# Plain products for the first four column blocks, longer load runs and spread weight copies in a Strassen-like ReGLU MLP

## The chip, the cores and the metric

The kernel runs on one core of one Trainium2 chip (trn2). The metric is the device time of a run in microseconds (us), lower is better; runs of one kernel agree within about 1%. The profiled execution of a kernel is one of its runs; its span is about 1.8 us shorter than that run's time. PE is TensorE, DVE is VectorE, ACT is ScalarE, POOL is GpSimd and SP is SyncE; PEclk is the granted TensorE clock, 1.0 being full speed. The views print 1.00 until the first change of clock that a trace records, so at the very start the matmul times tell more than PEclk. A load "lands" when its transfer has finished.

## The reference, cut to what matters

```python
# x: (16, 256, 512), w1: (512, 4096), w2: (2048, 512), all float32
h = x @ w1
gate, value = np.split(h, 2, axis=-1)
h = np.maximum(gate, 0) * value
return (h @ w2).astype(np.float32)
```

## The kernel before

The 4096 tokens go in four sets of 1024. A set is cut into two token halves (512 each); the 512 input features are cut into two halves; and w1 into gate and value. So the first layer is a 2 x 2 by 2 x 2 block product, done per column block of 128 hidden columns with seven products (P1 to P7) instead of eight. One product is two matmuls of 128x128 by 128x512. Its operands are sums: S1 to S4 of blocks of x, T1 to T4 of blocks of w1. A set has 16 such column blocks, and then the second layer: 8 output tiles of 16 matmuls. The last four matmuls of a set's second layer are spread into the next set's first blocks.

While the second layer of a set runs, x of the next set is loaded, transposed by DVE in 32x32 squares, and summed by POOL. This is where the change and the argument touch:

```python
stage = ctx.enter_context(tc.tile_pool(name="stage", bufs=3))    # x half tiles and w1 tiles, 4 KB each
tmp = ctx.enter_context(tc.tile_pool(name="tmp", bufs=4))
psx = ctx.enter_context(tc.tile_pool(name="psx", bufs=3, space=bass.MemoryType.PSUM))   # X and O
...
def load_x(s, h, k):                    # half a token half: 512 KB in four transfers, runs of 256 B
    t = stage.tile([P, 16, 64], F32, name="xs", tag="stage")
    for q in range(4):
        nc.sync.dma_start(out=t[q * 32:(q + 1) * 32], in_=x_v[s, h, k, q])
    return t

def turn(t):                            # reads t with a step of 2 floats (8 bytes)
    a = tmp.tile([P, 2, TH], F32, name="xt", tag="tmp")
    nc.vector.transpose(a.rearrange("p b (tb r) -> p b tb r", r=32),
                        t.rearrange("p tb (c b) -> p b tb c", b=2))
    return a

def x_ops(s, eng):
    o = x_tiles()
    t11 = load_x(s, 0, 0)
    t21 = load_x(s, 1, 0)
    yield o                             # each yield: ten matmuls of the second layer are issued
    a11 = turn(t11)
    nc.scalar.copy(out=o["A11"], in_=a11)
    t22 = load_x(s, 1, 1)
    yield o
    a21 = turn(t21)
    eng.tensor_tensor(o["S3"], a11, a21, op=SUB)
    t12 = load_x(s, 0, 1)
    yield o
    a22 = turn(t22)
    eng.tensor_tensor(o["S1"], a21, a22, op=ADD)
    nc.scalar.copy(out=o["A22"], in_=a22)
    yield o
    ...                                 # A12, S2, S4
...
def mm2_stream(s, g):                   # second layer
    for b in range(NB):
        ps = psx.tile([P, DO], F32, name="O", tag="X")
        for hc in range(NJ):
            nc.tensor.matmul(ps, g[:, hc, b * P:(b + 1) * P], w2_sb[:, hc, :],
                             start=hc == 0, stop=hc == NJ - 1)
            if hc < NJ - 1:
                yield
        o = tmp.tile([P, DO], F32, name="o", tag="tmp")
        nc.scalar.copy(out=o, in_=ps)   # in order on ACT, between the copies of x_ops
        nc.sync.dma_start(out=out_v[s, b], in_=o)
        yield
...
# opening: all of x_ops(0, ...) on DVE, w1 block 0 and 1 prepared, only then the first set's products
gen = x_ops(0, nc.vector)
xo = next(gen)
ws = {0: load_w1(0)}
next(gen)
w1_ops(0, ws[0], nc.vector)
for _ in gen:
    pass
...
```

The second layer's output tiles take their PSUM buffers from a pool of three (`psx`). A tile can start only when ACT has copied the tile three places before it. So whatever stands ahead of such a copy in ACT's queue can stop PE.

## Time and profile before

| Before | us |
|---|---|
| time, median (range) of 4 runs | 351.01 (350.92 to 352.05) |
| span of the profiled execution | 351.2 |
| sum of PE work without any wait: 64 blocks x 3.21 + 512 matmuls x 0.216 | 316 |
| start: until 26.0 us only 16 matmuls are done | 22 lost |
| two stops in blocks 11 and 12, and half clock until block 13 (counted from 0) | 8.7 lost |
| end: last matmul to end of span | 3.6 |

These are lines of the page of the kernel before. The first three are the busy tenths of PE, its granted clock and the DMA engines in 40 equal slices of 8.8 us. Then come groups of instructions (engine, operation, count, busy time, mean ns of one, idle time before them) and DMA issues (KB of one, median us from issue to landing).

```profile
PE   3259996799999999999999999999999999999995
PEclk9559999789999999999999999999999999999999
DMA  9957689920821700000821700000721000000212
...
L81 DVE STREAM_TRANSPOSE xt<-xs 128x1024 f32<-128x1024 f32 x16 | 19.5, 1234 | 25.0 <-DMA xs<-in_x_dram 17.6
...
xs<-in_x_dram SPq DMA_DIRECT2D x64, 128.0 KB, 3.3
...
w_sb<-in_w_dram POOLq DMA_DIRECT2D x4, 512.0 KB, 13.1
```

PE is short of work in the first three slices, around the seventh and eighth, and in the last. The view of waits, restricted to PE, names what ended each stop (total us, times, longest):

```profile
PE X L144 <- ACT Y L151: 9.2, 3, 4.0
PE W L144 <- DVE x_S_110 L104: 6.1, 1, 6.1
PE X L144 <- ACT w_B_81 L125: 4.0, 1, 4.0
```

Of the first line, one stop of 4.0 us lies at the start and two (2.97 and 2.25 us) in blocks 11 and 12 (the three slow blocks are 11 to 13 counted from 0; the prediction below calls them 10 to 12). The timeline of PE shows the start: start time, duration, instruction, and in brackets the idle time before it.

```profile
9.18 1.22 PE L144 MATMUL X<-x_A_107,w_B_81 128*128 128x512 f32 x2 [4.00 <-ACT w_B_81 L125]
16.47 1.19 PE L144 MATMUL W<-x_S_110,w_T_84 128*128 128x512 f32 x2 [6.07 <-DVE x_S_110 L104]
21.62 1.01 PE L144 MATMUL X<-x_A_108,w_B_82 128*128 128x512 bf16 x2 [3.96 <-ACT Y L151]
```

The first product runs at 9.18 us, the second must wait for S1 (a sum that needs A21 and A22), and the third for ACT's copy of the first one's result, which ran only at 20.99 us, behind copies of x and w1 in ACT's queue. Now the boundary between the first two sets, in the timeline of DVE. The second layer of the first set starts at 81.57 us.

```profile
85.58 2.36 DVE L81 STREAM_TRANSPOSE xt<-xs 128x1024 f32<-128x1024 f32 x2
92.25 1.25 DVE L81 STREAM_TRANSPOSE xt<-xs 128x1024 f32<-128x1024 f32 x1 [4.32 <-DMA xs<-in_x_dram]
```

A11 and A21 are both transposed at once, because both halves had been loaded long before. Only the third and fourth loads are issued here (87.41 us), and the third lands at 92.25. The output copies on ACT wait little, and PE has no gap at any boundary.

### The profile page before, as it was taken

The numbers are of one execution on the slowest core, as the hardware profiler recorded it, in microseconds if no ns is written. First come the engines' busy times: TensorE is split into PE (matmuls) and PEld (weight loads), VectorE is DVE, ScalarE is ACT, GpSimd is POOL, SyncE is SP. The second block draws the span as 40 slices with busy tenths as digits, with TensorE's granted clock in tenths as the row PEclk, the third lists the DMA queues.
The fourth block names the chain that finished last, engine by engine and source line by source line (L and its number), as shares of the span: only waits on it lengthen the run. The fifth ranks groups of instructions, "written<-read, shape, count | busy, mean of one in ns | idle before, by whom it ended". The sixth has DMA issues, their size and how long they took to land.

```text
span 351.2 us, 4077 instructions
## 1 busy us (share of the span) xinstructions
PE 326.3 (93%) x1416; PEld 204.5 (58%) x1416; DVE 195.1 (56%) x285; ACT 153.9 (44%) x285; POOL 71.7 (20%) x76
## 2 busy tenths in 40 slices
PE   3259996799999999999999999999999999999995
PEld 1137774575445777775445777775445777775442
DVE  2877786368201778778201788778111788776000
ACT  2277775443234455543233455543233455552121
POOL 0068996520540000000540000000460000000000
PEclk9559999789999999999999999999999999999999
DMA  9957689920821700000821700000721000000212
GB/s 164 194 156 201 184 181 213 205 62 0 179 105 46 149 0 3 0 1 2 179 96 55 149 0 0 2 1 0 182 97 54 32 0 0 0 2 0 91 68 81
DMA packets 57940, 27.53 MB, mean 78 GB/s; under 512 B 35392, under 2 KB 53824, under 8 KB 57920
## 3 DMA queue, kind: packets, MB, share of 16 engines
q1 hardware_dynamic: 55808, 25.18, 28.1%
q0 software_dynamic: 2112, 2.10, 3.6%
q8 instruction: 11, 0.18, 0.2%
q14 instruction: 9, 0.07, 0.1%
HBM read 20.97 MB, written 8.39 MB: 84 GB/s over the span
## 4 chain that ended last, share of the span: by engine, by line
PE 79%; DMA 7%; POOL 6%; SPq 3%; issue 2%; DVE 1%; ACT 0%; POOLq 0%; DVEq 0%; ACTq 0%
PE O L188 32%; PE Y L144 21%; PE W L144 14%; PE X L144 13%; DMA ws<-in_w_dram 7%; SPq L118 2%; POOL w_T_87 L131 1%; POOL w_T_85 L128 1%; POOL w_T_86 L130 1%; SPq L76 1%; POOL w_T_84 L126 1%; POOL w_sb L240 1%; DVE xt L81 1%; DVE x_S_110 L104 0%; ACT Y L151 0%
## 5 line engine op out<-in xcount | busy, mean ns | idle before, releaser
L188 PE MATMUL O<-w_sb,g 128*128 128x512 bf16 x512 | 113.6, 379 | 0.0
L171 DVE TENSOR_TENSOR cc<-W,pu 128x512 f32<-128x512 f32 x64 | 44.3, 692 | 89.6 <-ACT pu L165 82.6
L188 PEld LDWEIGHTS <-g 128*128 128x128 bf16 x512 | 48.7, 98 | 61.1 <-issue 4.9
L165 ACT COPY pu<-Y 128x512 f32<-128x512 f32 x64 | 37.6, 587 | 46.6 <-PE Y L144 46.6
L151 ACT COPY Y<-X 128x512 f32<-128x512 f32 x64 | 36.7, 574 | 43.6 <-PE X L144 43.6
L193 ACT COPY o<-O 128x512 f32<-128x512 f32 x32 | 18.8, 586 | 70.4 <-PE O L188 65.9
L172 DVE SCALAR_TENSOR_TENSOR g<-X,cc 128x512 bf16<-128x512 f32 x64 | 44.2, 691 | 2.4
L181 DVE SCALAR_TENSOR_TENSOR g<-Y,cc 128x512 bf16<-128x512 f32 x64 | 43.5, 680 | 3.4 <-PE Y L144 3.4
L177 DVE TENSOR_TENSOR cc<-Y,pu 128x512 f32<-128x512 f32 x64 | 43.6, 681 | 3.1 <-PE Y L144 3.1
L158 ACT COPY pu<-W 128x512 f32<-128x512 f32 x64 | 37.5, 586 | 0.5 <-PE W L144 0.3
L81 DVE STREAM_TRANSPOSE xt<-xs 128x1024 f32<-128x1024 f32 x16 | 19.5, 1234 | 25.0 <-DMA xs<-in_x_dram 17.6
L144 PEld LDWEIGHTS <-w_B_82 128*128 128x128 bf16 x128 | 7.9, 98 | 26.6 <-issue 25.9
L144 PE MATMUL X<-x_A_108,w_B_82 128*128 128x512 bf16 x32 | 10.1, 398 | 9.2 <-ACT Y L151 9.2
L144 PE MATMUL W<-x_S_110,w_T_84 128*128 128x512 f32 x32 | 11.4, 443 | 6.1 <-DVE x_S_110 L104 6.1
L100 POOL TENSOR_TENSOR x_S_1397<-xt 128x1024 fp32r<-128x1024 f32 x1 | 2.3, 2342 | 66.5 <-DVE xt L81 66.5
L100 POOL TENSOR_TENSOR x_S_2016<-xt 128x1024 fp32r<-128x1024 f32 x1 | 2.4, 2351 | 66.3 <-DVE xt L81 66.3
L126 POOL TENSOR_TENSOR w_T_84<-ws 128x256 fp32r<-128x256 f32 x14 | 10.4, 746 | 26.2 <-DMA ws<-in_w_dram 26.2
L144 PE MATMUL X<-x_A_107,w_B_81 128*128 128x512 f32 x32 | 11.8, 456 | 4.0 <-ACT w_B_81 L125 4.0
L144 PE MATMUL Y<-x_S_111,w_T_85 128*128 128x512 f32 x32 | 13.6, 506 | 0.0
L144 PE MATMUL Y<-x_S_777,w_T_85 128*128 128x512 f32 x32 | 13.0, 487 | 0.0
L144 PE MATMUL Y<-x_S_2015,w_T_85 128*128 128x512 f32 x32 | 13.0, 487 | 0.0
L144 PE MATMUL Y<-x_S_1396,w_T_85 128*128 128x512 f32 x32 | 13.0, 487 | 0.0
(92 smaller groups left out, 466.6 us busy)
## 6 DMA issues: line engine op xcount, KB each, us to landing
xs<-in_x_dram SPq DMA_DIRECT2D x64, 128.0 KB, 3.3
ws<-in_w_dram SPq DMA_DIRECT2D x64, 128.0 KB, 2.7
out_dram<-o SPq DMA_DIRECT2D x32, 256.0 KB, 2.0
w_sb<-in_w_dram POOLq DMA_DIRECT2D x4, 512.0 KB, 13.1
```

The lines of the kernel that those rows point to most:

```text
L81: nc.vector.transpose(a.rearrange("p b (tb r) -> p b tb r", r=32), t.rearrange("p tb (c b) -> p b tb c", b=2))
L126: eng.tensor_tensor(op["T1"], b12, b11, op=SUB)
L144: nc.tensor.matmul(ps, wop[wn][:, b, self.jb * P:(self.jb + 1) * P], self.xo[xn][:, b, :], start=fresh and b == 0, stop=b == 1, skip_group ...
L151: nc.scalar.copy(out=self.Y, in_=self.X)
L158: nc.scalar.copy(out=self.p5, in_=self.W)
L165: nc.scalar.copy(out=self.u2, in_=self.Y)
L171: nc.vector.tensor_tensor(self.c12, self.W, self.u2, op=ADD)
L172: nc.vector.scalar_tensor_tensor(out=self.g[:, self.jb, :TH], in0=self.X, scalar=0.0, in1=self.c12, op0=MAX, op1=MULT)
L177: nc.vector.tensor_tensor(self.c22, self.Y, self.p5, op=ADD)
L181: nc.vector.scalar_tensor_tensor(out=self.g[:, self.jb, TH:], in0=self.Y, scalar=0.0, in1=self.c22, op0=MAX, op1=MULT)
L188: nc.tensor.matmul(ps, g[:, hc, b * P:(b + 1) * P], w2_sb[:, hc, :], start=hc == 0, stop=hc == NJ - 1)
L193: nc.scalar.copy(out=o, in_=ps)
```

## The change

The intent: shorten the start. Four column blocks of the first set use the eight plain products, which need only copies of x and w1, so that PE can start as soon as half of x is there and the sums are made meanwhile. x comes in 1 MB loads of 512-byte runs and w1 in pairs of blocks with 1 KB runs; the first set's second x load is staged in the idle space of g, and w1 in the idle space of w2, so w2 must load after all of w1. 38 warm-up matmuls hold the clock until x is there. The last output tile is split between ACT and DVE. To make this fit, x staging shrinks to one buffer of 8 KB (a whole token half), and `x_ops` is rewritten for it.

```diff
-    stage = ctx.enter_context(tc.tile_pool(name="stage", bufs=3))
-    tmp = ctx.enter_context(tc.tile_pool(name="tmp", bufs=4))
+    stage = ctx.enter_context(tc.tile_pool(name="stage", bufs=1))
+    tmp = ctx.enter_context(tc.tile_pool(name="tmp", bufs=5))
...
-    x_v = x2.rearrange("(s h tb r) (k q c) -> s h k q r tb c", h=2, tb=16, r=32, k=2, q=4)
+    x_v = x2.rearrange("(s h tb r) (q c) -> s h q r tb c", h=2, tb=16, r=32, q=4)
...
-    def turn(t):
-        a = tmp.tile([P, 2, TH], F32, name="xt", tag="tmp")
+    def turn(a, t, k):
         nc.vector.transpose(a.rearrange("p b (tb r) -> p b tb r", r=32),
-                            t.rearrange("p tb (c b) -> p b tb c", b=2))
+                            t.rearrange("p tb (c k b) -> p k b tb c", k=2, b=2)[:, k])
         return a
+
+    def x_tile():
+        return stage.tile([P, 16, P], F32, name="xs", tag="xs")
...
         o = x_tiles()
-        t11 = load_x(s, 0, 0)
-        t21 = load_x(s, 1, 0)
+        t1 = load_x(s, 0, x_tile())
         yield o
-        a11 = turn(t11)
+        a11 = turn(x_tmp(), t1, 0)
         nc.scalar.copy(out=o["A11"], in_=a11)
-        t22 = load_x(s, 1, 1)
+        a12 = turn(x_tmp(), t1, 1)
+        nc.scalar.copy(out=o["A12"], in_=a12)
+        t2 = load_x(s, 1, x_tile())
         yield o
-        a21 = turn(t21)
+        a21 = turn(x_tmp(), t2, 0)
+        a22 = turn(x_tmp(), t2, 1)
+        eng.tensor_tensor(o["S1"], a21, a22, op=ADD)
         eng.tensor_tensor(o["S3"], a11, a21, op=SUB)
-        t12 = load_x(s, 0, 1)
-        yield o
-        a22 = turn(t22)
-        eng.tensor_tensor(o["S1"], a21, a22, op=ADD)
         nc.scalar.copy(out=o["A22"], in_=a22)
         yield o
...
+    class Plain:
+        def products(self, h, a1, a2):
+            ...
+            for a, gate, value in ((a1, "B11", "T3"), (a2, "T4", "B22")):
+                for ps, wn in ((X, gate), (W, value)):
+                    for b in range(2):
+                        nc.tensor.matmul(ps, wop[wn][:, b, js], a[:, b, :], start=a is a1 and b == 0,
+                                         stop=a is a2 and b == 1)
...
+    fetch(0, nc.scalar)
+    t1 = load_x(0, 0, x_tile())
+    fetch(1, nc.sync)
+    fetch(2, nc.sync)
+    t2 = load_x(0, 1, late)             # late: the space of g's blocks 12 to 15
+    ...
+    plain[0].products(0, r11, r12)
+    ...                                 # plain blocks 0 to 3 for half 0, then for half 1,
+    plain[3].products(1, r21, r22)      # with S1 to S4 (DVE) and T1 to T4 (POOL) made between them
```

## The prediction

> **What bounds it now.** TensorE: in the windows view it is busy without a gap from 110 us on. One block (14 products) takes 3.21 us in the timeline, one second-layer matmul 0.216 us (114 in 24.6 us in the chain of waits), so 64 blocks and 512 matmuls need about 64 x 3.21 + 512 x 0.216 = 316 us. The other 35 us:
> - start: by 26.0 us only 16 matmuls (3.7 us) are done: 22 us lost. PE waits for four x loads, transposes and sums, and for w1, all behind SP's issues, partly at half clock;
> - blocks 10 to 12: two stops behind a w1 load that took 12 us beside the w2 load (usually 2.7), then half clock: 18.3 us for three blocks, 8.7 lost;
> - end: last matmul at 347.6, then copy, issue, landing: 3.6 us.
>
> **What the change does.**
> 1. Plain blocks need only A11/A12, then A21/A22, and w1 copies: no sums before the first product. Cost: 64 matmuls instead of 56, fp32r at 0.231: +2.0 us; ideal 318 us.
> 2. First w1 on ACT's queue, x in 1 MB loads of 512-byte runs, w1 in 1 MB pairs of 1 KB runs. The first two loads are 1.5 MB; estimated at 200 to 250 GB/s (before: 199 at 512-byte runs, DMA share 0.7), landed by 7.5 to 9 us. Transpose 1.24 + copy 1.04: first operand at 10 to 11.5. The Trainium skill ("DMA: Bandwidth & Descriptors", Specifications) puts line rate at 512 bytes and up; the 256-byte x loads here ran at 218 GB/s with DMA share over 1, which agrees.
> 3. 38 warm-up matmuls from 2.0 us: some 9 at 0.427, 29 at about 0.22: until 12.2 us. The skill ("TensorE: Matmul & The Clock Gate", Part 1) has about 3.4 us of activity before full clock; the trace agrees (restart 21.6, full at 25.0). Real work starts near 12.4 us, warm.
> 4. w1 is staged in w2's space, so w2 loads after all w1: the 8.7 us stop goes. POOL needs an estimated 1.3 us per 128x512 operation (0.745 for 256, 2.35 for 1024 columns), 5.3 a pair, under PE's 6.4. w2 is issued at 54 to 57 us and lands by 70, just as the second layer needs it.
> 5. Last output in halves: 0.2 to 0.5 us.
>
> **New waits.** (a) Half 1 of the plain blocks needs the second x load, 4 MB into the queue (17 to 20 us), then transposes and copies: 0 to 3 us. (b) Copies of w1 pairs stand in ACT's queue and wait for loads whose buffer was just freed: 1 to 2 us around blocks 4 to 6. (c) At each set boundary x staging has one buffer: the second load starts after the first is transposed, and the A22 copy precedes the second output copy on ACT. PE needs that PSUM buffer 15 us after the second layer starts, the copy comes at about 16: 1 us, three times.
>
> **Sum.** 12.4 + 318 + 3.2 (end) + 2.5 (a, b, w2) + 3 (c) = 339 us, 3.4% faster; range 335 to 344. Faster by over 2%: 0.90; within 2%: 0.09; slower: 0.01.
>
> **Right if** the first plain product starts at 11.5 to 14 us at granted clock 1.0; set 1 starts near 97 us, not 109; no w1 landing of 12 us; no PE gap between 50 and 65 us; POOL's sums at a boundary end 23 us after the second layer starts.
>
> **Wrong if** warm-up ends before x has landed and the clock falls again; the longer runs load no faster; w2 comes late (each us after 70 adds one); the boundary waits are 3 us, or none.

## The result, and the profile after

The changed kernel is correct and slower. Its median is 367.5 us (366.71 to 369.32, 4 runs) against 351.01 us of the kernel before (4 runs): ratio 1.047, 95% interval 1.0426 to 1.0514. A ratio here is the mean time of one kernel's runs over the mean of the other's runs of the same rounds, so it is not quite the ratio of the two medians. The predicted 339 us, with a range of 335 to 344, was wrong, and on the wrong side of 351.

Here are the lines of the page of the changed kernel that answer to those shown before. Line L218 is the second layer, and L87 is the transpose.

```profile
PE   7969999996799999999499999999589999999995
PEclk9999999999699999999899999999969999999998
DMA  9973687905225000006132400001422000000212
...
L218 PE MATMUL O<-w_sb,g 128*128 128x512 bf16 x500 | 120.5, 396 | 16.6 <-ACT o L230 16.0
...
L87 DVE STREAM_TRANSPOSE xt<-xs 128x1024 f32<-128x1024 f32 x14 | 27.5, 2000 | 28.5 <-DMA xs<-in_x_dram 28.5
...
L227 DVE COPY o<-O 128x256 f32<-128x256 f32 x1 | 0.4, 425 | 25.2 <-ACT o L225 25.2
...
xs<-in_x_dram SPq DMA_DIRECT2D x28, 256.0 KB, 4.9
...
w_sb<-in_w_dram POOLq DMA_DIRECT2D x4, 512.0 KB, 9.2
```

The start is full but for the third slice (7 9 6, the waits of the plain blocks below), and it is warm (at full clock): the timeline has the first product at 13.00 us, and from 15.91 us on each pair of matmuls follows the one before by 0.46 us. The stop in the seventh and eighth slices of before is gone. But three dips have come, at slices 10-11, 20 and 29-30. They are the set boundaries. The second layer's group now has 16.6 us of idle time, before it had 0.0. One transpose takes 2.0 us where it took 1.24. The view of waits puts all the waiting at the boundaries on one line (16.0 us in three stops); the next two are the largest waits of the first set's plain blocks:

```profile
PE O L218 <- ACT o L230: 16.0, 3, 5.4
...
PE X L206 <- ACT x_A_182 L302: 1.3, 1, 1.3
PE X L206 <- ACT x_S_185 L299: 1.1, 1, 1.1
```

"ACT o" is the copy of an output tile, but that copy takes only 0.58 us. What it stood behind is told by the chain of waits through the first boundary (start, duration, what), followed back from a second-layer matmul:

```profile
77.90 4.04 DVE xt L87 x2
...
81.96 0.31 SPq L83
...
83.37 5.22 DMA xs<-in_x_dram
...
88.67 3.86 DVE xt L87 x2
...
92.56 1.05 ACT x_A_707 L116
...
93.64 0.46 ACT o L230
...
94.14 4.00 PE O L218 x9
```

Read from the top: the first x half, long landed, is transposed twice. Only then is the single staging buffer free, so the second load is issued at 81.96 and lands at 88.67. Two more transposes follow, then the copy of A22 on ACT, and only behind it, in ACT's queue, the copy of output tile 1. PE needed the buffer of that tile for output tile 4 at 88.93 and got it at 94.14: a gap of 5.21 us, in the timeline of PE:

```profile
94.14 15.70 PE L218 MATMUL O<-w_sb,g 128*128 128x512 bf16 x59 [5.21 <-ACT o L230]
```

In the windows view (stretch, its length, then busy us and count of PE, PEld, DVE, ACT and POOL, then clock, DMA share and GB/s) the clock falls late in the gap and is still at half after it (by the trace's clock record from 92.58 to 99.41 us):

```profile
90.00:92.00 2.00, 0.00 (x0) 0.00 (x0) 2.00 (x2) 0.00 (x0) 0.00 (x0) 1.00 0.00 0
92.00:94.20 2.20, 0.06 (x1) 0.06 (x1) 0.52 (x1) 1.53 (x2) 1.53 (x1) 0.63 0.00 0
94.20:96.00 1.80, 1.80 (x5) 0.63 (x5) 0.00 (x0) 0.58 (x1) 1.80 (x2) 0.50 0.39 146
96.00:98.00 2.00, 2.00 (x7) 0.66 (x5) 0.00 (x0) 0.58 (x1) 2.00 (x2) 0.50 0.35 131
```

The 59 matmuls that follow take 15.70 us, where 59 x 0.216 is 12.7. The other two boundaries have gaps of 5.38 and 5.39 us, and 59 matmuls in 14.78 and 15.98 us.

The loss can be added up from the times at which sets start. The table compares the stretches with those of before:

| Stretch (us) | Before | After |
|---|---|---|
| first product | 9.18 | 13.00 |
| start of the first set's second layer | 81.57 | 73.95 |
| from there to the start of set 1 | 27.63 (to 109.20) | 35.53 (to 109.48) |
| set 1 to set 2 | 79.18 (to 188.38) | 86.28 (to 195.76) |
| set 2 to set 3 | 79.01 (to 267.39) | 87.51 (to 283.27) |
| set 3 to the end of the span | 83.8 | 84.2 |

The change gains 7.6 us in the first set, and the three boundaries give back 7.9, 7.1 and 8.5 us, 23.5 in all. The first boundary alone uses up the gain.

### The profile page after: what moved, and what is told of

It is laid out like the page before. It is cut to its first block, busy times and chain, and to the rows that moved or that the text cites. A ratio compares the mean times of both kernels' runs of the same rounds, so it can differ in the third digit from the quotient of the medians.

```text
span 367.5 us, 3904 instructions
## 1 busy us (share of the span) xinstructions
PE 339.1 (92%) x1428; PEld 208.9 (57%) x1454; DVE 199.7 (54%) x270; ACT 151.1 (41%) x261; POOL 78.2 (21%) x58
## 4 chain that ended last, share of the span: by engine, by line
PE 72%; DMA 11%; DVE 7%; POOL 4%; ACT 2%; SPq 2%; issue 1%; DVEq 0%; ACTq 0%
PE O L218 23%; PE Y L153 22%; PE W L153 14%; PE X L153 13%; DVE xt L87 6%; DMA w_sb<-in_w_dram 6%; DMA xs<-in_x_dram 4%; SPq L83 2%; POOL w_T_84 L135 1%; POOL w_T_85 L136 1%; POOL w_T_87 L138 1%; POOL w_T_86 L137 1%; ACT o L230 0%; ACT w_B_82 L270 0%; ACT x_A_1925 L116 0%
## 5 line engine op out<-in xcount | busy, mean ns | idle before, releaser
L218 PE MATMUL O<-w_sb,g 128*128 128x512 bf16 x500 | 120.5, 396 | 16.6 <-ACT o L230 16.0
L218 PEld LDWEIGHTS <-g 128*128 128x128 bf16 x512 | 50.3, 101 | 83.0 <-issue 31.3
L180 DVE TENSOR_TENSOR cc<-W,pu 128x512 f32<-128x512 f32 x60 | 41.5, 691 | 97.8 <-ACT pu L174 96.0
L160 ACT COPY Y<-X 128x512 f32<-128x512 f32 x60 | 34.3, 572 | 49.7 <-PE X L153 43.3
L87 DVE STREAM_TRANSPOSE xt<-xs 128x1024 f32<-128x1024 f32 x14 | 27.5, 2000 | 28.5 <-DMA xs<-in_x_dram 28.5
L181 DVE SCALAR_TENSOR_TENSOR g<-X,cc 128x512 bf16<-128x512 f32 x60 | 41.5, 691 | 2.3
L190 DVE SCALAR_TENSOR_TENSOR g<-Y,cc 128x512 bf16<-128x512 f32 x60 | 40.8, 680 | 3.3 <-PE Y L153 3.3
L186 DVE TENSOR_TENSOR cc<-Y,pu 128x512 f32<-128x512 f32 x60 | 40.9, 681 | 0.8 <-PE Y L153 0.3
L153 PEld LDWEIGHTS <-w_B_82 128*128 128x128 bf16 x120 | 7.2, 98 | 16.6 <-issue 15.9
L227 DVE COPY o<-O 128x256 f32<-128x256 f32 x1 | 0.4, 425 | 25.2 <-ACT o L225 25.2
L153 PE MATMUL Y<-x_S_1318,w_T_85 128*128 128x512 f32 x32 | 13.0, 487 | 0.0
L153 PE MATMUL Y<-x_S_709,w_T_85 128*128 128x512 f32 x32 | 13.0, 487 | 0.0
L153 PE MATMUL Y<-x_S_1927,w_T_85 128*128 128x512 f32 x32 | 13.0, 486 | 0.0
L135 POOL TENSOR_TENSOR w_T_84<-w_sb 128x512 fp32r<-128x512 f32 x6 | 8.7, 1456 | 8.6 <-DMA w_sb<-in_w_dram 8.6
L153 PE MATMUL X<-x_A_1314,w_B_81 128*128 128x512 f32 x32 | 10.3, 404 | 0.0
L153 PE MATMUL X<-x_A_1923,w_B_81 128*128 128x512 f32 x32 | 10.3, 404 | 0.0
L153 PE MATMUL X<-x_A_705,w_B_81 128*128 128x512 f32 x32 | 10.3, 403 | 0.0
```

The lines of the kernel that those rows point to most:

```text
L135: nc.gpsimd.tensor_tensor(op["T1"], b12, b11, op=SUB)
L153: nc.tensor.matmul(ps, wop[wn][:, b, self.jb * P:(self.jb + 1) * P], self.xo[xn][:, b, :], start=fresh and b == 0, stop=b == 1, skip_group ...
L160: nc.scalar.copy(out=self.Y, in_=self.X)
L180: nc.vector.tensor_tensor(self.c12, self.W, self.u2, op=ADD)
L181: nc.vector.scalar_tensor_tensor(out=self.g[:, self.jb, :TH], in0=self.X, scalar=0.0, in1=self.c12, op0=MAX, op1=MULT)
L186: nc.vector.tensor_tensor(self.c22, self.Y, self.p5, op=ADD)
```

## The experiments

Eight kernels ran beside the kernel before: the first four together on one chip (before: median 351.25 us), the other four together in a second job (before: median 351.2 us). Ratios are against the kernel before. Differences from the changed kernel's 367.5 us, and between the two jobs, are between medians of different jobs; the kernel before, at 351.01, 351.25 and 351.2 us, shows that the jobs compare.

The theory of the boundary: the chain above is a series of four transposes, a load that can't be issued early, and a copy, and it ends about 5 us too late; a gap this long also costs half clock. The rivals: the order of ACT's queue alone is to blame; or the second layer itself became slower; or the slow transposes are all of it.

### e1_stride: transposes at 1.2 us

The Trainium skill ("SBUF — State Buffer", Specifications) says that SBUF has cachelines of 16 bytes and that full bandwidth needs at least two hits on each. The new `turn` steps through x by four floats, 16 bytes, so each read is in a new line; the old one stepped by 8 bytes. This experiment gives the transposes a step of 4 and 8 bytes, with everything else unchanged. The features are then permuted wrongly, so the result is wrong.

```diff
-                            t.rearrange("p tb (c k b) -> p k b tb c", k=2, b=2)[:, k])
+                            t.rearrange("p tb (k b c) -> p k b tb c" if k == 0 else
+                                        "p tb (k c b) -> p k b tb c", k=2, b=2)[:, k])
```

> Only the order in which the transposes read x is changed (wrong results on purpose): the first half is read at unit stride, the second at a stride of 8 bytes, in place of 16. Theory A (the 16-byte stride makes each transpose 2.0 us instead of 1.24, and the boundary chain has four of them): both forms fall to about 1.2 us, the second output copy of each boundary ends 2.9 us earlier, PE idles about 2.3 us there instead of 5.2 to 5.4 and its clock does not fall afterwards; 350 to 354 us. Rival B (the transposes are slow for another reason, such as the larger staging tile or loads in flight): they stay at 2.0 us and the time at 367.

Measured: 353.38 us (352.62 to 354.26), ratio 1.0053 (1.0027 to 1.0078). This is 14.1 us less than the changed kernel. These are the groups of DVE and the waits of PE:

```profile
L87 DVE STREAM_TRANSPOSE xt<-xs 128x1024 f32<-128x1024 f32 x14 | 16.6, 1221 | 28.4 <-DMA xs<-in_x_dram 28.4
```

```profile
PE O L219 <- ACT o L231: 6.7, 3, 2.4
```

The step size is the cause of the slow transposes: 2000 ns become 1221 ns, with the staging tile and the loads as before. (That cachelines are the reason is the skill's account; the run shows the effect of the step.) Four of them on the chain are 4 x 0.78 = 3.1 us less per boundary, and the gaps fall from 5.2, 5.4 and 5.4 to 2.42, 2.15 and 2.10 us. What is left is the load, issued at 80.31 and landed at 87.38. The slow matmuls go too, at two of three boundaries: the 60 matmuls after the gaps took 14.79, 13.11 and 13.11 us. So the clock still fell after the gap of 2.42 us, against the expectation. The first set gained nothing: its second layer starts at 73.99, as in the changed kernel. In this run it also had a gap of 1.86 us (20.01 to 21.87) and half clock from 23.10 to 26.51, which the changed kernel's first set had not. So the slow transposes are most of the boundary, but not all of it.

### e2_oneload: no second load at the boundaries

The second token half of sets 1 to 3 is taken from the first load (wrong result). The transposes stay slow. If the late load is a necessary link of the chain, the gaps must go.

```diff
-        t2 = load_x(s, 1, x_tile())
+        t2 = t1
```

> The second x load of sets 1 to 3 is left out and the first tile is transposed twice (wrong results on purpose); the transposes stay slow. Theory A (the second load can start only after the first tile is transposed, because there is one staging buffer): the second output copy comes about 13.5 us after the second layer starts, PE needs it at 15, so there is no PE gap at a boundary and no half clock: 343 to 347 us. Rival C (the tmp buffers or ACT's order hold the output copies whatever the load does): 3 to 5 us of gap remain at each boundary, 355 us or more.

Measured: 345.36 us, ratio 0.9833 (0.9812 to 0.9855). The timeline of PE shows the whole second layer of the first set in one piece, and the group of DVE shows that the transposes are still slow:

```profile
76.89 24.78 PE L218 MATMUL O<-w_sb,g 128*128 128x512 bf16 x114
```

```profile
L87 DVE STREAM_TRANSPOSE xt<-xs 128x1024 f32<-128x1024 f32 x14 | 27.4, 2026 | 7.5 <-DMA xs<-in_x_dram 7.5
```

Without the load all three gaps are gone, and 22.1 us with them (367.5 to 345.36). That is the whole boundary loss of 23.5 us but for 1.4. The 114 matmuls take 24.78 us, the same as in the kernel before, so the second layer itself has not become slower. The slow transposes are harmless then. They and the load stand in one series, and e1 and e2 each shorten that series, so their savings overlap and can't be added.

### e3_a22late: the A22 copy behind the output copies

The rival says that it is only the place of one copy in ACT's queue.

```diff
         eng.tensor_tensor(o["S3"], a11, a21, op=SUB)
-        nc.scalar.copy(out=o["A22"], in_=a22)
         yield o
...
         yield o
+        nc.scalar.copy(out=o["A22"], in_=a22)
```

> Only the A22 copy of sets 1 to 3 moves: on ACT it now follows the second and third output copies. Rival C (ACT's order is the cause): the gap goes, 344 to 348 us. Theory A (the late second load is the cause, and the third output copy needs a tmp buffer that POOL's sums free only after it): the second output copy is early, but the gap moves to the next output tile with about the same length: 363 to 369 us.

Measured: correct, 368.39 us, ratio 1.048 (1.0443 to 1.0516): no gain. The waits of PE, and the output copy that PE waited for at the first boundary:

```profile
PE O L218 <- ACT o L230: 17.4, 3, 5.9
```

```profile
97.91 0.59 ACT L230 COPY o<-O 128x512 f32<-128x512 f32 x1 [14.05 <-POOL x_S L115]
```

The gap moved by one output tile and grew. The output copy that PE needs now waited for a sum of POOL (14.05 us for S3 at the first boundary, by the timeline of ACT), which itself needs the late A21. Output copies take their tiles from the pool that holds the transposed x, which would explain that wait; this was not tested apart. Taking the copy away from one place in the queue does not help when the operands behind it are as late as before.

### e4_oldbound: the new opening with the old boundary

If the opening is good and the boundary is bad, the two should be separable. This kernel keeps the plain blocks, the warm-up, w1 in w2's space and w2 after w1, but has the half tiles, 256-byte runs, 8-byte steps and the order of loads of before at the boundaries. x staging has two buffers of 4 KB (the space of the one of 8 KB); the first set's x is staged in the idle space of g.

```diff
-    stage = ctx.enter_context(tc.tile_pool(name="stage", bufs=1))
+    stage = ctx.enter_context(tc.tile_pool(name="stage", bufs=2))
...
-    x_v = x2.rearrange("(s h tb r) (q c) -> s h q r tb c", h=2, tb=16, r=32, q=4)
+    x_v = x2.rearrange("(s h tb r) (k q c) -> s h k q r tb c", h=2, tb=16, r=32, k=2, q=4)
...
-        t1 = load_x(s, 0, x_tile())
+        t11 = load_h(s, 0, 0, h_tile())
+        t21 = load_h(s, 1, 0, h_tile())
         yield o
...                                     # the rest of x_ops as in the kernel before
-        eng.dma_start(out=t, in_=w1_v[:, :, jb * P:(jb + n) * P])
+        for k in range(2):
+            eng.dma_start(out=t[:, 4 * k:4 * k + 4], in_=w1_v[k, :, :, jb * P:(jb + n) * P])
...
+    t11 = load_h(0, 0, 0, g_space(0))  # t12, t21, t22 the same in g_space(1), (2), (3)
```

> The new opening with the boundary of the kernel before: x in half tiles of 256-byte runs, two in staging, transposes at a stride of 8 bytes, sums in the old order. Theory A: no PE gap at the boundaries; the opening keeps its gain of about 8 us (set 1 at 109.5 minus 8 lost at the boundary, against 109.2 before), and faster transposes add 1 to 2: 340 to 345 us, faster than both kernels. Rival D (the opening itself gains nothing: 8 more products and w1 waits eat it): 349 us or more.

Measured: correct, 342.75 us (341.41 to 344.08), ratio 0.9753 (0.9713 to 0.9793). It beats both kernels. Set 1 starts at 98.97 us, and PE has no gap at the boundary:

```profile
74.54 24.78 PE L222 MATMUL O<-w_sb,g 128*128 128x512 bf16 x114
```

So the opening is worth 8.5 us (351.25 to 342.75), where the prediction had 12 for the whole change, and the changed kernel loses all of it at the boundaries. It also shows one part of the opening that does not matter. The x loads here have 256-byte runs, and the first product still starts at 12.66 us, right behind the warm-up (e7 below, with a short warm-up, starts it at 9.85); the longer x runs were not needed for it. The x half tile that is needed first lands sooner here (its transpose starts at about 7.5 us; in the changed kernel, where the first load is a whole token half, at 9.73).

### e5_fill: the clock's share of the loss

The changed kernel with 22 useless matmuls ahead of the fifth output tile, so that PE is busy in the gap. The gap's own time can't come back; the half clock after it can.

```diff
             ps = psx.tile([P, DO], F32, name="O", tag="X")
+            if b == 4 and not last:
+                for i in range(22):
+                    if i % 8 == 0:
+                        d = psy.tile([P, TH], F32, name="Y", tag="Y")
+                    nc.tensor.matmul(d, w2_sb[:, 0, :P], w2_sb[:, 1, :], start=True, stop=True,
+                                     skip_group_check=True)
```

> The changed kernel, with 22 matmuls of no use (4.75 us at full clock, into an idle PSUM bank) put before the fifth output tile of each set but the last, where PE waits 5.2 to 5.4 us. Theory A (the 2 to 3 us lost after each gap are PE's clock, which falls in the gap): the clock stays at 1.0 and the matmuls after the gap take 0.216 us again; the wait itself stays; 359 to 362 us. Rival E (the slow stretch after the gap has another cause, such as output copies or stores): 366 to 369 us.

Measured: correct, 362.47 us, ratio 1.0326 (1.0292 to 1.0359): 5.0 us less than the changed kernel. The timeline of PE:

```profile
89.18 4.91 PE L221 MATMUL Y<-w_sb 128*128 128x512 bf16 x22
94.46 13.11 PE L224 MATMUL O<-w_sb,g 128*128 128x512 bf16 x59 [0.37 <-ACT o L236]
```

The 59 matmuls take 13.11 us at each of the three boundaries, instead of 15.70, 14.78 and 15.98. That is 7.1 us in all, and the two profiled spans differ by 6.7 (367.5 and 360.8). The medians differ by less, 5.0 us, and the profiled execution of the changed kernel is the slowest of its four runs, with the clock lower than in two of the others (mean 0.974 against 0.981). So the half clock is worth 5 to 7 us of the 23.5, and the rest is waiting.

### e6_onesbuf: DVE and POOL in the first set

The first set lost more than predicted too. In the changed kernel, POOL's sums of w1, 512 columns each, should take 1.3 us, but four of the first eight took 2.24 to 2.29. These lines of the timelines of the changed kernel are the second to fourth sum of POOL's first pair, and then DVE's S1 (L300) in the same stretch:

```profile
23.74 1.26 POOL L136 TENSOR_TENSOR w_T_85<-w_sb,w_T_84 128x512 fp32r<-128x512 f32 x1
24.97 2.26 POOL L137 TENSOR_TENSOR w_T_86<-w_sb 128x512 fp32r<-128x512 f32 x1
27.19 1.30 POOL L138 TENSOR_TENSOR w_T_87<-w_sb,w_T_85 128x512 fp32r<-128x512 f32 x1
```

```profile
24.04 2.05 DVE L300 TENSOR_TENSOR x_S_183<-xt 128x1024 fp32r<-128x1024 f32 x1
```

DVE's S2 took 2.14 us too, and S4 1.21. The Trainium skill ("SBUF — State Buffer", Who interferes with whom) says that a DVE instruction with two SBUF inputs contends with a GpSimd instruction that reads SBUF, through a port pair that one of them holds for its whole instruction. The theory: they wait for each other. S1 starts at 24.04 while POOL's sum runs until 25.00, and ends 1.1 us after that, at 26.09; POOL's next sum starts at 24.97 and ends 1.1 us after S1, at 27.23. The rival: the POOL operations are slow because of DMA traffic or their operands. The test, on the base of e4: S1 to S4 of the first set are computed with one operand from PSUM (a tile of zeros, so the result is wrong).

```diff
+    zero = psy.tile([P, TH], F32, name="Y", tag="Y")
+    nc.tensor.matmul(zero, warm_b[:, :P], warm_b[:, :TH], start=True, stop=True)
+    def one_input(out, a, op):
+        for b in range(2):
+            nc.vector.tensor_tensor(out[:, b, :], a[:, b, :], zero, op=op)
...
-    nc.vector.tensor_tensor(xo["S1"], a21, a22, op=ADD)
+    one_input(xo["S1"], a22, ADD)
...                                     # S2, S3, S4 likewise
```

> The kernel of e4, but the four sums of the first set on DVE read one operand from PSUM instead of two from SBUF (wrong results on purpose). Theory F (a DVE sum with two SBUF operands and a POOL operation hold each other up: in e4 four POOL operations took 2.3 us instead of 1.29 while such a sum ran, and this delays the w1 chain of the first set): all POOL operations take 1.29 us, the first second-layer matmul starts at 70 to 71 us instead of 71.4, total 341 to 342.5. Rival: POOL's times do not change.

Measured: 341.28 us (340.03 to 343.22), ratio 0.973 (0.9684 to 0.9777). The same two sums in the timelines of POOL, first of e4, then of this run:

```profile
25.68 2.27 POOL L141 TENSOR_TENSOR w_T<-w_sb 128x512 fp32r<-128x512 f32 x1
27.91 1.29 POOL L142 TENSOR_TENSOR w_T<-w_sb,w_T 128x512 fp32r<-128x512 f32 x1
```

```profile
24.14 1.29 POOL L141 TENSOR_TENSOR w_T<-w_sb 128x512 fp32r<-128x512 f32 x1
25.40 1.29 POOL L142 TENSOR_TENSOR w_T<-w_sb,w_T 128x512 fp32r<-128x512 f32 x1
```

All twelve POOL sums from 21.3 to 37 us took 1.28 to 1.30 us. So the second SBUF operand of DVE's sums is the cause of the long ones; that a port lock stands behind it is the skill's account, which fits. The run also cuts each of DVE's sums in two, but shortness is not the cure: in the kernel before, DVE sums of 256 columns with two SBUF operands took 0.83 to 0.94 us beside POOL's sums (20.22 to 22.77 us), and 0.42 at 10.40 us, when POOL stood still. What the lock is worth in time is not resolved: the medians differ by 1.5 us, but the intervals of e4 and e6 overlap. In the profiled executions the second layer starts at 68.60 us instead of 71.41, sooner than expected, but e4 had half clock from 23.54 to 26.96 us there, which alone costs some 1.7 us (estimate: half of 3.41), and e6 had none.

### e7_warm8: a short warm-up

On the base of e4, 8 warm-up matmuls instead of 38. The question is whether the long warm-up, which holds PE until 12.6 us, pays.

```diff
-NWARM = 38
+NWARM = 8
```

> The kernel of e4 with 8 warm-up matmuls instead of 38. If the long warm-up is what lets the first products run at full clock, they run at half clock for about 3.4 us from 12.7 us on: 1.7 to 2.5 us more, 344 to 345.5. Rival: the first products wait for loads anyway and take it up: 342 to 343.

Measured: correct, 343.65 us, ratio 0.9792 (0.9766 to 0.9818). That is 0.9 us above e4, and not resolved. It lies between the range that was expected and that of the rival, just outside both. The timeline of PE:

```profile
9.85 1.22 PE L210 MATMUL X<-x_A,w_B 128*128 128x512 f32 x2 [4.26 <-ACT x_A L297]
...
17.67 0.63 PE L210 MATMUL X<-x_A,w_B 128*128 128x512 f32 x2
```

The first product could start at 9.85 us, 2.8 us before the warm-up of e4 lets it. But it starts cold (at half clock): pairs of matmuls follow each other by 0.86 us, and by 0.46 from 17.67 us on. PEclk reads 1.00 here, because the trace records no change of clock before the rise to full at 17.38 us. The two nearly cancel: the long warm-up is worth about nothing, because it goes on for 2.8 us after x is ready.

### e8_poolq: the second x load from another queue

On the base of e4, SP issues eight transfers for the second x half, about 1 us each (9.19 to 17.09 us), ahead of a w1 load that POOL's first sum then waits for until 22.01. Here POOL issues the second x half instead.

```diff
-    t21 = load_h(0, 1, 0, g_space(2))
-    t22 = load_h(0, 1, 1, g_space(3))
...
+    t21 = load_h(0, 1, 0, g_space(2), nc.gpsimd)   # after plain_w(0)
...
+    t22 = load_h(0, 1, 1, g_space(3), nc.gpsimd)   # after plain_w(1)
```

> The kernel of e4, but the second x tile of the first set is issued from POOL's queue instead of SP's, so that SP can issue the w1 load of blocks 4 and 5 at about 13 us instead of 17.1. Theory G (the first set's remaining loss of about 7 us is the chain SP issues, w1 load, POOL): POOL's first difference starts 3 us earlier, second layer at 69 to 70.5 us, total 339.5 to 341.5. Rival: loads from POOL's queue come later or slow the others down: 342 or more.

Measured: correct, 343.93 us, ratio 0.9807 (0.9768 to 0.9847): no gain over e4. The expectation is missed; the rival's 342 or more came true. POOL's first sum starts at 20.96, only 1 us sooner, and the copies of the second x half come later: PE waits 2.7 us in the plain phase (in e4 1.5), and the second layer starts at 73.94 instead of 71.41. Moving the issue does not make the loads faster; it only changes which one is late.

## Why the prediction was wrong, point by point

The prediction's sum was 12.4 + 318 + 3.2 + 2.5 + 3 = 339. The same terms as measured in the profiled execution:

| Term | Predicted | Measured | How |
|---|---|---|---|
| first plain product | 12.4 | 13.0 | timeline |
| PE work | 318 | 318 | same durations of matmuls |
| (a), (b), w2: first set | 2.5 | 7.6 | plain phase 13.00 to 32.33 is 19.3 against 64 x 0.231 = 14.8; twelve blocks, 32.33 to 73.95, are 41.6 against 12 x 3.21 = 38.5 |
| (c) boundaries | 3 | 23.5 | differences of set starts, above |
| end | 3.2 | 3.9 | last matmul 363.6, span 367.5 |
| sum | 339 | 366.0 | 1.5 us of the span of 367.5 are not assigned |

**The step that failed is new wait (c), "1 us, three times".** Its mechanism was named rightly: one staging buffer, the second load behind the first transposes, and the A22 copy ahead of an output copy on ACT. Its size was wrong, 23.5 us instead of 3, and by itself it turns the prediction's gain into a loss. The prediction had the needed copy 16 us after the second layer starts, against a need at 15; the copy came at 20.1 (94.09 - 73.95). Two things made it so late, and a third made the lateness dearer:

- A transpose was priced at 1.24 us, the duration in the trace of before. But the change had altered what the transposes read: the step went from 8 to 16 bytes. They took 2.0 us, and four stand on the chain: 3 us. e1 shows that the step is the cause, and that these 3 us per boundary make 14.1 us of time: 9.3 in the three gaps (16.0 to 6.7), and most of the rest in matmuls at half clock.
- The second load took 6.7 us from issue to landing (81.96 to 88.67). The prediction gives no figure for it; with transposes of 1.24 us and the rest of the chain as measured, a copy at 16 leaves it about 5.5. e2 shows that this load is a necessary link.
- The fall of the clock after a gap was not in the sum. The prediction itself quoted the warm-up of about 3.4 us, but applied it to the start only. e5 shows that it is worth 5 to 7 us in all.

A margin was the real risk here. Need at 15 and supply at 16 was a difference of two sums of several durations each; two kinds of them were too small, and each microsecond of lateness cost more than a microsecond, three times.

**(a), (b) and w2: wrong by 5.1 us.** The second x half landed at 19.49, within the predicted 17 to 20. The plain blocks of half 1 then waited three times, 0.4 to 1.3 us, for copies and for DVE. "5.3 a pair" for POOL was wrong while DVE made S1 to S4: the first two pairs took 6.1 and 8.1 us, because of the meeting of the two engines that e6 takes away. The chain of waits from 3 to 42 us runs through w1 loads and POOL's sums, not through x. How much of the 5.1 us is due to the lock is open. So is the share of the slow transposes: e1, which has fast ones, gained nothing in the first set, but it lost time to half clock there.

**The end: no gain.** 3.9 us instead of 3.2 (before: 3.6). DVE's half copy began at 364.08, when ACT's half (363.68 to 364.05) was over, so the two copies did not run side by side; the group line of L227 above names ACT as what DVE waited for. Why it must wait was not tested.

**What was right.** The first plain product at 13.0 and at full pace (predicted 11.5 to 14). After the start no w1 load took more than 7.4 us to land (before: 12.0 in the stop); but one of those of the start took 11.0. Between 50 and 65 us there was one PE wait of 0.4 us, and the stops of 2.97 and 2.25 are gone. w2 was issued from 59 us (predicted 54 to 57) and landed in 9.2 us (median), the last part at about 73.6 instead of 70, just before the second layer at 73.95; PE did not wait for it. The opening is worth its work: e4, which keeps it and undoes the boundary, is 2.5% faster than before, and lies in the predicted range. Two other signs that the prediction named failed with step (c): set 1 starts at 109.48 us, not near 97, and POOL's sums at the first boundary end 28.1 us after the second layer starts, not 23.

**What was right for another reason than stated.** The loads of the start did run faster (308 GB/s from 10 to 15 us, where the kernel before had at most 218 in a 5-us window of the start). But e4 has 312 GB/s in that window with 256-byte x runs and 1 KB w1 runs. So the longer x runs, which cost the second staging buffer and the step of the transposes, were not what brought the speed or the early start. The 512-byte threshold that the prediction quoted from the skill was not tested by itself.

**Open.** Why the first set in e4 still begins its second layer at 71.41 us (68.60 in e6); how far the lock, the 1.51 us gap at 23 us, and the half clock after it share that. Whether a version with both repairs of the first set and a shorter warm-up gains more than the noise of about 1.5 us was not run.

## What to carry to other kernels

When a change alters the layout that an instruction reads, do not price that instruction from the old trace: ask what its innermost step in bytes was and is. When a change takes away a buffer, write down the whole chain that now runs in series, compare its end with the moment at which the busiest engine needs it, and if the margin is near zero, count the case that it is missed, with the clock that falls after it, times the number of repetitions. And test the parts of a bundled change apart: here a good opening was hidden by a boundary that had been rewritten only to make room for it.

## What the Trainium skill lacked or had wrong

- "SBUF — State Buffer", note on cachelines in the section on the port swizzle ("Door 1"): it says that one can stride for free by 4 fp32. Here a DVE transpose of 128x1024 fp32 with a step of 4 fp32 took 2.00 us, with a step of 2 fp32 1.24 us, and with unit and 2-fp32 steps in e1 a mean of 1.22 us. The other rule of the same page (two hits per 16-byte line) agrees with this. The page gives no size for the penalty; here it is a factor of 1.6.
- "SBUF — State Buffer", Who interferes with whom: it agrees with the runs, but has no size for fp32 sums. A POOL sum of 128x512 went from 1.29 to 2.27 us and a DVE sum of 128x1024 from 1.21 to 2.05 and 2.14 us when the two met; with one operand in PSUM (e6) all twelve POOL sums took 1.28 to 1.30.
- "TensorE: Matmul & The Clock Gate", Part 1: it puts the fall to half clock after at least one idle window of about 3.4 us, and says that the window is free-running. The clock records of the traces here agree with the free-running window: in every run all changes of clock lie whole multiples of 3.413 us apart (the changed kernel: down at 92.58, up at 99.41, down at 181.33, up at 184.74, down at 266.66, up at 273.49 us; so the loss after a gap comes in steps, two windows, one and two). What the page lacks is how much of a window must be idle. A whole one is not needed: gaps of 2.97 and 2.25 us (the kernel before), 2.42 and 1.86 us (e1, first boundary and first set) and 1.51 us (e4) were followed by half clock, while gaps of 2.15 and 2.10 us (e1) and of 1.08 and 1.30 us (the changed kernel) were not. Where the gap falls matters too: the one of 2.42 us (88.94 to 91.36) lay inside the window that ended at 91.37, and the one of 2.15 us (172.23 to 174.38) was split by the end of a window at 173.29 (counted on from 91.37 in steps of 3.413).
